# Two one-column buffers fewer, and what lies behind them in a partition moves down by 64 bytes

## The chip, the cores and the metric

The kernel runs on one core of a Trainium2 chip. The metric is the time on the device in microseconds (us) of one execution, for a program that is launched once. Before the change three runs gave 2437.39, 2440.98 and 2445.57 us; the median is 2440.98 us. A profile was taken of one execution, which took 2439.48 us by itself, and its span from the first to the last instruction is 2437.7 us.

## What is computed

The reference is one step of a hybrid encoder with one layer: 2048 prompt tokens and 8 x 16 sample tokens of width 1024, all in float32.

```python
def trunk_layer(x, ...):
    u = rms_norm(x, norm_mix) @ w_in                 # 1024 -> 2564 columns for four mixers
    ya, ... = mixer_ssd(...)                         # chunked state-space scan
    yb      = swa_prompt(...) or swa_sample(...)     # banded attention
    yc, ... = mixer_shortconv(...)
    yd, ... = mixer_conformer(...)                   # 31-tap convolution, layer norm
    x = x + concatenate([ya, yb, yc, yd]) @ w_out
    hf = rms_norm(x, norm_ffn)
    x = x + (silu(hf @ w_gate) * (hf @ w_up)) @ w_down     # 1024 -> 2816 -> 1024
    return x, states
y = rms_norm(x, norm_final)
```

## The kernel before

**Tiles.** The tokens lie along the free axis, the features on the 128 partitions. The 2176 tokens are worked in five chunks of 256, 512, 512, 384 + 128 (the samples) and 384 tokens. Every projection (w_in, w_out, gate, up, down) is a row of matmuls of a 128 x 128 block of weights against an operand of 128 partitions by one chunk.

**Precision.** Weights and operands are split into a high and a low part of a 32-bit type made for matmuls (`split_w` at L202, `split` at L197): ScalarE copies the high part (L204, L199), VectorE subtracts it and leaves the low part (L184). Each product of a block is then three matmuls: high weights times high operand (L239), high weights times low operand (L240), low weights times high operand (L241). TensorE loads its weights anew for each of the three.

**Stages.** Chunks 0 to 2 run through w_in, the mixers, w_out and the feed-forward layer one after the other; the mixers of a chunk are woven between the projections of its neighbours, and the order of instructions on each engine comes from a scheduler that reads the program with its buffers and priorities. The feed-forward layer of chunks 3 and 4 is done together at the end for two halves of 448 tokens (`N` = 448) with seven products in place of eight (`quad`, L1146, and `product`, L1137, whose three matmuls are L1141 to L1143); I call this the quad stage. The products by `w_down` that follow run through `product` too (L1280 and L1292); I call this the down stage.

**Buffers.** Tiles come out of pools with a number of buffers for each tag. The pools on the left of a partition are laid out one behind the other: `cp` (tables, constants and small sums), then `wp` (the raw weights `fr` and the split weights `w`), then the mixer pools `up` and `mp`, in whose place `gp` and `xp` (tiles `g` and part of the operands `hf`) stand at the end of the program. The operands `act`, `h`, `ht`, the rest of `hf` (pool `xq`) and the working tiles `nt`, `ft`, `x2` lie in pools on the right, which are laid out from the other end. A buffer of one column of float32 takes 32 bytes of a partition.

**The place of the change.** `norm1_stats` (L302) makes the sum of squares of a chunk's tokens before its first projection. For chunks 1 to 4 it loads 128 tokens in two halves of 512 features (SyncE, L333), squares them on ScalarE with a sum along the row (L334), and adds the second half's sum `part` to the first's on VectorE (L336; in a profile it stands under the helper's line L184, as `n<-n,n` with one column). `part` is a tile of tag `n1`; `sums` is one of tag `n8`. Each `n1` buffer is free again once its addition has run. This is side work: `weave` puts it among the projections of other chunks.

Of the kernel before, what the change touches and what calls it, by code (L numbers as in the profile page):

```python
# [17 lines left out]
P = 128  # L18
# [100 lines left out]
def stream_step(ctx: ExitStack, tc: tile.TileContext, cfg, x, xr, w_in, w_out, w_gu, w_down, tab, con, dist_p, dist_s,  # L119
# [7 lines left out]
    cp = ctx.enter_context(tc.tile_pool(name="cp", bufs=1))  # L127
# [15 lines left out]
    def mk(pool_, shape, tag, dt=F32, **kw):  # L143
        uid[0] += 1
        return pool_.tile(shape, dt, tag=tag, name=f"{tag}_{uid[0]}", **kw)
# [37 lines left out]
    def tt(out, a, b, op, eng=dve):  # L183
        return eng.tensor_tensor(out=out, in0=a, in1=b, op=op)  # L184
# [59 lines left out]
    def newton(v, r, t, src, n):  # L244
        ts(v, src, 1.0 / n, ALU.mult, EPS, ALU.add)

        ts(r.bitcast(I32), v.bitcast(I32), 1, ALU.logical_shift_right)
        ts(r.bitcast(I32), r.bitcast(I32), -1.0, ALU.mult, float(0x5F1FFFF9), ALU.add)
        stt(t, v, -0.703952253, r, ALU.mult, ALU.mult)
        tt(t, t, r, ALU.mult)  # L250
        stt(r, t, 0.703952253 * 2.38924456, r, ALU.add, ALU.mult)

        stt(t, v, 0.375 ** 0.5, r, ALU.mult, ALU.mult)
        tt(t, t, r, ALU.mult)
        stt(t, t, -1.25 / 0.375 ** 0.5, t, ALU.add, ALU.mult)
        stt(r, t, 1.875, r, ALU.add, ALU.mult)

    def rstd_of(sq, T, n, r=None):

        nb = T // P  # L260
        v, r_, t = (mk(cp, [P, 8], "n8", bufs=9)[:, :nb] for _ in range(3))
        r = r_ if r is None else r
        pc = mk(px, [P, 512], "px")
        for b in range(nb):
            pe.matmul(pc[:, b:b + 1], sq[:, b * P:(b + 1) * P], ones[:, 0:1], start=True, stop=True)
        newton(v, r, t, pc[:, :nb], n)
        return r
# [34 lines left out]
    def norm1_stats(c):  # L302
        T, o = c["T"], c["off"]
        hold = c["i"] == 0 and KT * T <= 4 * TM
        if hold:
            ss = mk(np_, [P, TM], "ns", bufs=1)[:, :T]

            c["x"] = []
            sq = []
            with tc.high_priority(offset=8 * AHEAD):  # L310
                xs = [mk(ap, [P, 2, KT // 4, T], "act") for _ in range(2)]
                for j in range(4):
                    sync.dma_start(xs[j // 2][:, j % 2], x[:, 2 * j:2 * j + 2, o:o + T])
                    c["x"] += [xs[j // 2][:, j % 2, k] for k in range(KT // 4)]
                qs = [mk(ap, [P, 2, KT // 4, T], "act") for _ in range(2)]
                for j in range(4):
                    sq.append(qs[j // 2][:, j % 2])
                    act.activation(sq[j], xs[j // 2][:, j % 2], AF.Square)
                for q in sq[1:]:
                    tt(sq[0], sq[0], q, ALU.add)  # L320
                tt(ss, sq[0][:, 0], sq[0][:, 1], ALU.add)
            yield
            c["r1"] = rstd_of(ss, T, D)
            yield
            return

        nb = T // P
        sums = mk(cp, [P, 8], "n8", bufs=9)[:, :nb]
        for b in range(nb):
            for h in range(2):  # L330
                xt = mk(np_, [P, TM], "nt", bufs=B["nt"])
                part = mk(cp, [P, 1], "n1", bufs=4) if h else sums[:, b:b + 1]
                sync.dma_start(xt, xr[o + b * P:o + (b + 1) * P, h * 512:(h + 1) * 512])  # L333
                act.activation(xt, xt, AF.Square, accum_out=part)  # L334
                if h:
                    tt(sums[:, b:b + 1], sums[:, b:b + 1], part, ALU.add)  # L336
            if b % 2:
                yield
        if nb % 2:
            yield  # L340
        v, r, t = (mk(cp, [P, 8], "n8", bufs=9)[:, :nb] for _ in range(3))
        newton(v, r, t, sums, D)
        c["r1"] = r
        yield
# [620 lines left out]
    def stats1(c):  # L965
        g = norm1_stats(c)
        return twice(g, (c["T"] // P + 1) // 2 + 1)
# [35 lines left out]
    for t in twice(norm1_stats(chunks[0])) + twice(norm1(chunks[0]), 4):  # L1003
        run(t)
# [428 lines left out]
```

## Time and profile before

| what | value |
|---|---|
| median of three runs | 2440.98 us (2437.39 to 2445.57) |
| the profiled execution's own time | 2439.48 us |
| its span, first to last instruction | 2437.7 us |
| mean granted TensorE clock | 0.988 |
| busy: VectorE, ScalarE, GpSimd | 65%, 36%, 6% of the span |
| bytes from and to memory | 324.07 MB read, 91.18 MB written |

A matmul's line in the profile gives the shape of its operand, its count and the mean duration of one. Matmuls overlap: one begins long before the one ahead has ended, so the duration of one (401 ns at 512 columns) is not what it costs. What it costs is the step from one start to the next, which I call the **pace**. It is read from the starts in the timeline, or from a stretch without gaps and the number of matmuls in it.

### The profile page before, as it was taken

The page shows a single profiled execution, that of the slowest core. Times are in us where ns is not written, and L with a number is a line of the kernel's source. Part 1 is how long each engine was busy: PE and PEld are TensorE (multiplying, and loading weights), DVE is VectorE, ACT ScalarE, POOL GpSimd, SP SyncE. Part 2 cuts the span into 40 slices and gives each one's busy share as a digit, 9 for nine tenths or more (in the row PEclk, how much of TensorE's full clock was granted, in tenths as well). Part 3 has the DMA queues.
Part 4 walks back from the last instruction along what each step waited for, and adds up shares of the span by engine and source line. Part 5 has one row for each costly group of instructions (what it writes and reads, how often), then busy time and mean ns, then how long its engine had stood idle before and what let it go on. Part 6 is the DMA issues. An engine that isn't in the chain of part 4 may idle for free.

```text
span 2437.7 us, 32296 instructions
## 1 busy us (share of the span) xinstructions
PE 2373.2 (97%) x12350; PEld 2036.4 (84%) x12350; DVE 1584.0 (65%) x2988; ACT 882.3 (36%) x1494; POOL 146.9 (6%) x266
## 2 busy tenths in 40 slices
PE   6999999999999999997999999999999999999997
PEld 6788999887877778886877788988879999999997
DVE  7897998855784446656573454675687667663324
ACT  5545555533333233323222222233334444442221
POOL 0000000000000000001000000000001000000000
PEclk9999999999999999998999999999999999999998
DMA  6547445567554554555434336653633332338653
GB/s 217 182 163 245 149 156 163 168 234 282 181 185 154 191 173 160 199 208 155 163 135 149 138 121 222 218 172 115 207 108 134 113 130 93 120 121 311 209 186 119
DMA packets 133179, 417.37 MB, mean 171 GB/s; under 512 B 12848, under 2 KB 49616, under 8 KB 115872
## 3 DMA queue, kind: packets, MB, share of 16 engines
q1 hardware_dynamic: 115248, 324.57, 41.1%
q0 software_dynamic: 17776, 90.73, 9.7%
q8 instruction: 97, 1.59, 0.3%
q14 instruction: 58, 0.48, 0.1%
HBM read 324.07 MB, written 91.18 MB: 170 GB/s over the span
## 4 chain that ended last, share of the span: by engine, by line
PE 52%; DMA 2%; DVE 1%; ACT 0%; issue 0%; DVEq 0%; POOL 0%; ACTq 0%; POOLq 0%
PE pm L239 8%; PE pm L240 8%; PE pm L241 8%; PE pm L1141 7%; PE pm L1143 7%; PE pm L1142 7%; PE px L1143 1%; PE px L1141 1%; PE px L1142 1%; DMA o_xc_s<-raw 1%; DVE x L187 0%; DMA act<-kc 0%; DMA raw<-xst 0%; PE px L675 0%; DMA w<-kept 0%; PE px L703 0%
## 5 line engine op out<-in xcount | busy, mean ns | idle before, releaser
L239 PE MATMUL pm<-act,w 128*128 128x512 f32 (+2 forms) x2216 | 808.3, 365 | 6.7 <-ACT act L199 4.1
L240 PE MATMUL pm<-act,w 128*128 128x512 f32 (+2 forms) x2216 | 800.0, 361 | 10.3 <-DVE act L184 10.3
L241 PE MATMUL pm<-act,w 128*128 128x512 f32 (+2 forms) x2216 | 800.0, 361 | 2.3 <-DVE w L184 2.2
L204 ACT ACTIVATE w<-fr 128x1024 fp32r<-128x1024 f32 (+2 forms) x380 | 393.8, 1037 | 909.0 <-PE pm L241 512.4
L184 DVE TENSOR_TENSOR w<-fr,w 128x1024 fp32r<-128x1024 f32 (+2 forms) x380 | 454.2, 1196 | 295.4 <-ACT w L204 294.5
L239 PEld LDWEIGHTS pm<-act,w 128*128 128x128 f32 x2216 | 419.8, 190 | 77.5 <-ACT act L199 5.7
L240 PEld LDWEIGHTS pm<-act,w 128*128 128x128 f32 x2216 | 419.9, 190 | 73.8 <-DVE act L184 11.5
L241 PEld LDWEIGHTS pm<-act,w 128*128 128x128 f32 x2216 | 419.6, 189 | 66.9 <-DVE w L184 3.3
L1141 PE MATMUL pm<-hf,w 128*128 128x448 f32 x616 | 226.2, 367 | 0.0
L1142 PE MATMUL pm<-hf,w 128*128 128x448 f32 x616 | 225.0, 365 | 0.0
L1143 PE MATMUL pm<-hf,w 128*128 128x448 f32 x616 | 224.9, 365 | 0.0
L187 DVE SCALAR_TENSOR_TENSOR mix<-raw,tabh,mix 128x384 f32<-128x384 f32 (+3 forms) x360 | 202.7, 593 | 2.1
L239 PE MATMUL pm<-h,w 128*128 128x512 f32 (+1 forms) x528 | 193.9, 368 | 7.3 <-ACT hf L199 3.3
L240 PE MATMUL pm<-h,w 128*128 128x512 f32 (+1 forms) x528 | 190.7, 362 | 0.1
L241 PE MATMUL pm<-h,w 128*128 128x512 f32 (+1 forms) x528 | 190.6, 362 | 0.0
L184 DVE TENSOR_TENSOR x<-x,pm 128x512 f32<-128x512 f32 (+2 forms) x184 | 107.9, 600 | 76.6 <-PE pm L241 68.8
L187 DVE SCALAR_TENSOR_TENSOR ft<-ft,pm 128x512 f32<-128x512 f32 (+1 forms) x132 | 78.6, 595 | 110.4 <-PE pm L241 91.1
L1143 PEld LDWEIGHTS pm<-hf,w 128*128 128x128 f32 x616 | 115.6, 188 | 10.6
L1141 PEld LDWEIGHTS pm<-hf,w 128*128 128x128 f32 x616 | 115.7, 188 | 9.8 <-ACT g L1155 0.2
L239 PEld LDWEIGHTS pm<-h,w 128*128 128x128 f32 x528 | 101.0, 192 | 27.1 <-ACT hf L199 3.7
L1142 PEld LDWEIGHTS pm<-hf,w 128*128 128x128 f32 x616 | 115.7, 188 | 9.4
L240 PEld LDWEIGHTS pm<-h,w 128*128 128x128 f32 x528 | 101.4, 192 | 16.7 <-issue 0.7
(288 smaller groups left out, 2554.0 us busy)
## 6 DMA issues: line engine op xcount, KB each, us to landing
w<-kept SPq DMA_DIRECT2D x83, 1024.0 KB, 5.2
fr<-w_gu SPq DMA_DIRECT2D x154, 512.0 KB, 3.3
kept<-w POOLq DMA_DIRECT2D x51, 1024.0 KB, 6.4
fr<-w_down SPq DMA_DIRECT2D x84, 512.0 KB, 3.8
fr<-w_in SPq DMA_DIRECT2D x52, 512.0 KB, 4.0
fr<-w_out SPq DMA_DIRECT2D x40, 512.0 KB, 3.4
hm<-h POOLq DMA_DIRECT2D x44, 448.0 KB, 4.4
ht<-hm SPq DMA_DIRECT2D x40, 448.0 KB, 5.3
```

The source lines that it names most:

```text
L184: return eng.tensor_tensor(out=out, in0=a, in1=b, op=op)
L187: return eng.scalar_tensor_tensor(out=out, in0=a, scalar=s, in1=b, op0=op0, op1=op1)
L204: act.activation(d[:, 0, :n], raw, AF.Copy)
L239: pe.matmul(ps[:, :T], wh, o[:, 0, :T], start=(i == 0), stop=False)
L240: pe.matmul(ps[:, :T], wh, o[:, 1, :T], start=False, stop=False)
L241: mm = pe.matmul(ps[:, :T], wl, o[:, 0, :T], start=False, stop=(i == n - 1))
L1141: pe.matmul(ps[:, :N], wh[:, i], a, start=first and i == 0, stop=False, skip_group_check=True)
L1142: pe.matmul(ps[:, :N], wh[:, i], b, start=False, stop=False, skip_group_check=True)
L1143: mm = pe.matmul(ps[:, :N], wl[:, i], a, start=False, stop=(i == n - 1), skip_group_check=True)
```

## The change

```diff
@@ norm1_stats, L332
-                part = mk(cp, [P, 1], "n1", bufs=4) if h else sums[:, b:b + 1]
+                part = mk(cp, [P, 1], "n1", bufs=2) if h else sums[:, b:b + 1]
```

Tag `n1` has two buffers in place of four. That does two things.

**First, every pool behind it on the left begins 64 bytes earlier in each partition**; the right side stays. By the addresses that the build gives the tiles, the beginnings modulo 512 bytes are:

| tile | before | after |
|---|---|---|
| weights `w`, raw weights `fr` | 32 | 480 |
| operands `act`, `h`, `ht`, `hf` of pool `xq` | 480 | 480 |
| operands `hf` of pool `xp` (row blocks 0 and 1 of 4) | 32 | 480 |
| mixer tiles `ut`, `k`, `mix`, `b2` and others | 96 | 32 |

A block of weights is 512 bytes long in a partition, so all blocks of a tile begin at the tile's own place. The low part of an operand lies 2048 bytes behind the high part where a tile holds 512 columns, which is the same place, and 1792 bytes behind it where it holds 448, which is 256 bytes further modulo 512. So before the change the weights and the operands of the first three chunks' projections and of the down stage were 64 bytes apart modulo 512; in the quad stage this held for half of the operands, and the other half began where the weights begin. After it, all of them begin at one place (the low parts at 448 columns 256 bytes off).

**Second, the third partial sum of a chunk must wait for the first addition.** TensorE's, GpSimd's and SyncE's rows are the same as before. On ScalarE one row moves, in the statistics of chunk 4, which run beside the w_in projections of chunk 3 and the feed-forward layer of chunk 2. The two pieces show ScalarE there; `nt_1689` is the working tile of the third block, `n1_1690` its partial sum, `pk` and `ut_1584` belong to the time steps of the scan, `w` are weights, `h` and `ft` belong to the feed-forward layer, and `ut_1603` is the projection v on its way to a transpose.

```order
 L199 ACTIVATE h_1581_10260<-ft_1577_10226 128x512 [waits DVE_49]
 L475 ACTIVATE ut_1584_10306<-pm_1583_10281,tab_1_84 128x512 [waits PE_49]
-L334 ACTIVATE nt_1689_11083,n1_1690_11084<-nt_1689_11083 128x512 [waits DMAHW5_49,Activation_49]
 L476 ACTIVATE ut_1585_10307<-ut_1584_10306 128x512 [waits Activation_49]
 L477 ACTIVATE ut_1585_10307<-ut_1585_10307 128x512 [waits Activation_49]
```

The square of the third block stood ahead of the chain of the time steps; here it is gone, and a few rows further down on the same engine it comes again:

```order
 L199 ACTIVATE h_1597_10430<-ft_1591_10367 128x512 [waits DVE_49]
 L911 ACTIVATE ft_1600_10460<-pm_1599_10435 128x512 [waits DVE_49,PE_49]
+L334 ACTIVATE nt_1689_11083,n1_1690_11084<-nt_1689_11083 128x512 [waits DMAHW5_49,DVE_49]
 L204 ACTIVATE w_1615_10585<-fr_1614_10583 128x1024 [waits DMAHW3_49,DMAHW4_49,DMAHW2_49,PE_49]
 L534 ACTIVATE ut_1603_10506<-pm_1602_10481 128x512
```

It now stands ahead of the split of the weights `w_1615` and of the copy of v, and waits for VectorE, which must have run the addition of the first partial sum. On VectorE, in the same place of the program, the additions of the first two partial sums stand just above the next piece, in both kernels at the same rows; that of the third moves down:

```order
 L368 COPY raw_1670_10953<-hg1_14_104 128x30
 L191 TENSOR_SCALAR raw_1670_10953<-raw_1670_10953 128x8x30
-L184 TENSOR_TENSOR n8_1647_10813<-n8_1647_10813,n1_1690_11084 128x1
 L368 COPY raw_1710_11210<-hs0_11_101 128x2
 L192 TENSOR_SCALAR mix_1672_10963<-raw_1670_10953,tabh_5_92,tab_1_84 128x128
+L187 SCALAR_TENSOR_TENSOR mix_1672_10963<-raw_1670_10953,tabh_5_92,mix_1672_10963 128x128
+L184 TENSOR_TENSOR n8_1647_10813<-n8_1647_10813,n1_1690_11084 128x1
+L187 SCALAR_TENSOR_TENSOR mix_1672_10963<-raw_1670_10953,tabh_5_92,mix_1672_10963 128x128
 L192 TENSOR_SCALAR n8_1726_11340<-n8_1647_10813 128x3
```

The third addition comes three rows later. Elsewhere on VectorE some taps of a convolution and steps of the scan change places among themselves. In the statistics of the other chunks the square of a later block now waits for an addition as well, at an unchanged place in the order.

## The prediction

> **What bounds the kernel now.** I read the page first, for which engine is full:
>
> ```profile
> span 2437.7 us, 32296 instructions
> PE 2373.2 (97%) x12350; PEld 2036.4 (84%) x12350; DVE 1584.0 (65%) x2988; ACT 882.3 (36%) x1494; POOL 146.9 (6%) x266
> PE   6999999999999999997999999999999999999997
> PEclk9999999999999999998999999999999999999998
> ```
>
> TensorE (PE) is busy in nearly every slice at nearly its full granted clock; nothing else comes near. The table of waits says the same from the other side:
>
> ```profile
> ACT w L204 <- PE pm L241: 512.4, 162, 11.4
> ```
>
> The split of the weights waits 512 us in all for TensorE to give a buffer back, so weights come early. Next, the groups by line with shapes kept apart, for how many matmuls of each width there are:
>
> ```profile
> L239 PE MATMUL pm<-act,w 128*128 128x512 f32 x1400 | 561.8, 401 | 4.6 <-ACT act L199 2.9 <-DMA w<-kept 1.7
> L239 PE MATMUL pm<-h,w 128*128 128x512 f32 x352 | 143.3, 407 | 3.3 <-ACT hf L199 3.3
> L239 PE MATMUL pm<-act,w 128*128 128x384 f32 x232 | 79.4, 342 | 0.0
> L239 PE MATMUL pm<-act,w 128*128 128x256 f32 x584 | 167.0, 287 | 2.1 <-ACT act L199 1.2 <-ACT w L204 0.5 <-ACT pk L498 0.4
> L239 PE MATMUL pm<-h,w 128*128 128x256 f32 x176 | 50.6, 290 | 4.0 <-DVE ft L187 1.8 <-DVE x L184 1.7 <-ACT h L199 0.5
> L1143 PE MATMUL pm<-hf,w 128*128 128x448 f32 x616 | 224.9, 365 | 0.0
> L1143 PE MATMUL px<-ht,w 128*128 128x448 f32 x160 | 58.8, 368 | 0.0
> L1143 PE MATMUL pm<-ht,w 128*128 128x448 f32 x160 | 58.8, 367 | 0.0
> L1143 PE MATMUL pm<-h,w 128*128 128x448 f32 x16 | 5.9, 366 | 0.0
> L1143 PE MATMUL px<-h,w 128*128 128x448 f32 x16 | 5.8, 365 | 0.0
> ```
>
> Each line has two sisters with the same count (L240 and L241, L1141 and L1142). So there are 3 x (1400 + 352) = 5256 matmuls of 512 columns, 696 of 384, 2280 of 256, 1848 of 448 in the quad stage and 3 x 352 = 1056 of 448 in the down stage. Idle time ahead of them is a few us in all.
>
> Last, seven gapless stretches, by the view of windows: start and end, the length, TensorE busy, the number of matmuls that it touches, clock, DMA share and GB/s. A window also counts a matmul that still runs at its left edge; the steps from its first to its last start are 354, 95, 22, 133, 60, 479 and 1653.
>
> ```profile
> 562.14:644.74 82.60, 82.60 (x356) 1.00 0.62 221
> 1528.36:1545.14 16.78, 16.78 (x97) 1.00 0.70 201
> 1601.22:1605.03 3.81, 3.81 (x23) 1.00 0.61 252
> 169.38:184.48 15.10, 15.10 (x136) 1.00 0.43 140
> 336.34:343.40 7.06, 7.06 (x62) 1.00 0.47 155
> 2214.03:2310.89 96.86, 96.86 (x480) 1.00 0.79 262
> 1866.83:2203.85 337.02, 337.02 (x1654) 1.00 0.36 120
> ```
>
> Length by steps gives the paces: 512 columns 233.3 ns; 384 columns 176.6 in one stretch and 173.2 in another; 256 columns 113.5 and 117.7; 448 columns 202.2 in the down stage and 203.9 in the quad stage. So one width has **two paces** at the same clock. Counts by paces (with the mean of the two at 384 and 256) give 1226 + 122 + 264 + 377 + 214 = 2203 us, 90% of the span. A change of pace goes to the end of the kernel whole.
>
> **The change part by part.** The sum is made against the profiled execution's own 2439.5 us, which lies 1.5 us under the median of the runs.
>
> *The wait on ScalarE* (chunk 4's statistics). These rows of the timeline are of ScalarE, VectorE and TensorE in turn:
>
> ```profile
> 1149.37 0.63 ACT L334 ACTIVATE nt<-nt 128x512 f32<-128x512 f32 x1 [3.57 <-DMA nt<-xr]
> ...
> 1172.67 1.06 ACT L204 ACTIVATE w<-fr 128x1024 fp32r<-128x1024 f32 x1 [2.49 <-PE pm L241]
> 1173.63 0.58 ACT L534 ACTIVATE ut<-pm 128x512 f32<-128x512 f32 x1
> ```
>
> ```profile
> 1173.95 0.23 DVE L184 TENSOR_TENSOR n<-n,n 128x1 f32<-128x1 f32 x2
> ```
>
> ```profile
> 1174.34 0.38 PE L543 MATMUL px<-con,ut 128*128 128x128 f32 x2
> ```
>
> The square that moves (first row) will stand just ahead of the split at 1172.67 and wait for the first of the two additions, which begins at 1173.95 and is done by about 1174.1. VectorE's rows up to there are as many as before, so that time stays. The square holds ScalarE 0.63 us; the split begins at about 1174.75, **2.1 us late**, and the copy of v behind it as late. TensorE takes v's transposes at 1174.34, 0.13 us after the copy ends (1173.63 + 0.58), so it will stand for 2.1 us, and all behind it in its queue moves. The split itself is of weights two units on, which hides it. ScalarE gains 3.57 + 0.63 us at 1149 in exchange, but TensorE had no gap there to give back:
>
> ```profile
> 1134.91:1174.10 39.19, 39.19 (x169) 1.00 0.63 209
> ```
>
> 168 steps at 233.3. Ends of the term: 0 (VectorE comes earlier by the 2.1) and 2.1; I take +2.1. The other added waits cost nothing: there the addition two sums back is done before the square begins, by the places of both in the order.
>
> *The place of weights and operands at 448 columns.* The quad stage has both cases side by side: in each product the first six matmuls take operands that begin where the weights begin (pool `xp`), the last six take operands 64 bytes apart (`xq`). The starts of the 1st, 7th and of the next product's 1st matmul:
>
> ```profile
> 1900.66 0.37 PE L1141 MATMUL pm<-hf,w 128*128 128x448 f32 x1
> ...
> 1901.90 0.37 PE L1141 MATMUL pm<-hf,w 128*128 128x448 f32 x1
> ...
> 1903.11 0.37 PE L1141 MATMUL pm<-hf,w 128*128 128x448 f32 x1
> ```
>
> 1.24 us for six at one place, 206.7 ns each; 1.21 us for six 64 apart, 201.7. Over the whole stretch: the mean is 203.9, and if the half that is 64 apart goes at the down stage's 202.2 (all 64 apart there), the other half goes at 205.6. Against it stands the very first quad, 1826.00 to 1842.78:
>
> ```profile
> 1826.00 0.36 PE L1141 MATMUL pm<-hf,w 128*128 128x448 f32 x1
> ...
> 1827.21 0.36 PE L1141 MATMUL pm<-hf,w 128*128 128x448 f32 x1
> ...
> 1828.42 0.36 PE L1141 MATMUL pm<-hf,w 128*128 128x448 f32 x1
> ```
>
> Here both halves take 1.21 us: one place can also go at the fast pace. So the place doesn't force the slow pace; it allows it, and which it is was set by what stood before the stretch. After the change all 448-wide matmuls are at one place. I take 205.6, since 1653 steps show it and the fast stretch has some 80: 1848 x (205.6 - 203.9) + 1056 x (205.6 - 202.2) = 3.1 + 3.6 = **+6.7 us**. Ends: all at 202.2, -3.1 us; all at 206.7, 5.2 + 4.8 = +10 us.
>
> *The place at 512, 384 and 256 columns.* All of these are 64 apart before, at one place after; no row shows that. The fast paces lie on a line: 113.5, 173.2, 233.3, some 60 ns for each 128 columns. The slow ones lie on another: 117.7, 176.6, and at 448 it gives 206.1, which is what one place showed there. So 512 columns go on the fast line now, and the slow line would be 235.5 there, +2.2 ns. Below, I bound by the step between the two paces at 256, -4.2; above by +4.2. That is from -22 to +22 us for 5256 matmuls, and at 256 from -9.6 to +9.6 for 2280; 384 has under 700 and is within 2 us. I take **0**: the row nearest to a 512-wide matmul is its own width's, and both long stretches of it quoted here, 570 us apart, have this one pace.
>
> A rule to weigh here: the Trainium skill, "SBUF — State Buffer", section "Who interferes with whom", gives TensorE two independent read ports, one for the operand and one for the weights; I read it as saying that it doesn't matter where the two lie. By it the term of place would be 0 and the sum 2441.6; the 206.7 against 201.7 above speaks against it, the 1.21 against 1.21 for it.
>
> Sum: 2439.5 + 2.1 + 6.7 + 0 = **2448.3 us**.
>
> **The rivals.**
>
> *All widths take the slow line.* If one place lets the slow pace in at every width as at 448, 512 columns pay 2.2 x 5256 = 11.6 us and 256 columns half of their 9.6, 4.8 us: 2448.3 + 16.4 = 2464.7. For it: the line fits three widths to 0.5 ns. Against it: the slow pace also occurs at 256 and 384 columns, 64 apart, so it isn't the place alone that makes it.
>
> *Place plays no part.* Then the two paces come from what stood ahead of a stretch alone, as the first quad suggests, and only the wait is left: 2439.5 + 2.1 = 2441.6. Against it: 1653 steps in a row with the two halves of each product apart.
>
> *One place is faster* (the other side). The weights of the next matmul are read while the operand of this one streams; if at one place the two run past each other with one delay less in each matmul, 512 columns gain what lies between the two paces at 256, 4.2 x 5256 = 22.1 us, 256 columns half of their 9.6, and 448 columns go at 202.2 (-3.1): 2441.6 - 22.1 - 4.8 - 3.1 = 2411.6. For it: 202.2 at 448 is already 1 ns under the fast line (203.3), so a place can do better than the line. Against it: no stretch at one place does better than 202. It decides from a gain of 0.9 ns on each 512-wide matmul (4.8 us), with the other terms at 2.1 - 3.1.
>
> **How the numbers follow.** Forecast 0.30, slow line at all widths 0.25, no part 0.20, one place faster 0.25. Against the median 2441.0, 0.3% is 7.3 us, which is about what a measurement of this kernel can tell from no change: under 2433.7 is faster, over 2448.3 slower. The forecast lies on that line, so I halve it: faster 0.25, same 0.20 + 0.15 = 0.35, slower 0.25 + 0.15 = 0.40. All terms at their low ends give 2405, all at their high ends 2483; with a tenth left out at each side the range is 2411 to 2474.
>
> **What would show it.** In the profile after: the pace at 448 columns in the quad stage and the down stage, about 205.6 in both if I am right, 202 if the place plays no part; the pace of the long 512-wide stretch near 562 us, 233.3 by the forecast, 235.5 by the slow line, 229 by the fast rival; a stand of about 2 us ahead of the transposes L543 near 1174 us. What would make me wrong most is the 512-wide pace: each 1 ns of it is 5.3 us, and no row of before shows it at one place.

## The result, and the profile after

| | before | after |
|---|---|---|
| median of four runs each | 2439.18 us (2436.48 to 2445.57) | 2417.66 us (2412.88 to 2418.89) |
| the profiled execution's own time | 2439.48 us | 2412.88 us |
| its span | 2437.7 us | 2411.1 us |

The ratio of after to before is 0.9904, 95% interval 0.9880 to 0.9929. The change makes the kernel faster by about 1%; I had forecast 2448.3 us, 0.3% slower. The time lies inside the range that I gave, near its lower end, on the side of the third rival. The profiled execution after the change is the fastest of its four: the two profiled executions lie 26.6 us apart, the medians 21.5, and what follows accounts for the profiled two. One execution of k3_both_lower below, at a granted clock of 0.654, took 3327.78 us and is in no ratio.

The page of the kernel after, the same four lines as before:

```profile
span 2411.1 us, 32296 instructions
PE 2343.1 (97%) x12350; PEld 2038.6 (85%) x12350; DVE 1582.2 (66%) x2988; ACT 882.4 (37%) x1494; POOL 147.3 (6%) x266
PE   6999999999999999998999999999999999999997
PEclk9999999999999999998999999999999999999998
```

TensorE (PE) still bounds the kernel in nearly every slice at the same clock, and the counts are the same. Of the busy times only its own has shrunk by more than 2 us, by 30.1. So the time went out of the matmuls themselves. The groups by line with shapes kept apart say which:

```profile
L239 PE MATMUL pm<-act,w 128*128 128x512 f32 x1400 | 553.1, 395 | 5.0 <-ACT act L199 3.2 <-DMA w<-kept 1.7
L239 PE MATMUL pm<-act,w 128*128 128x256 f32 x584 | 169.0, 291 | 1.8 <-ACT act L199 1.1 <-ACT w L204 0.4 <-ACT pk L498 0.3
```

At 512 columns the mean fell from 401 to 395 ns, at 256 it rose from 287 to 291. The paces are read from gapless stretches by the view of windows (start and end, length, TensorE busy, matmuls touched, clock, DMA share, GB/s), at least one of each width. The first and the sixth are those of 82.60 and 337.02 us before. From the first start to the last there are 354, 155, 94, 187, 83, 1653 and 479 steps:

```profile
564.26:644.55 80.29, 80.29 (x356) 1.00 0.63 226
166.11:184.71 18.60, 18.60 (x157) 1.00 0.44 142
405.08:416.36 11.28, 11.28 (x96) 1.00 0.55 184
1682.97:1715.40 32.43, 32.43 (x189) 1.00 0.64 208
1824.07:1841.21 17.14, 17.14 (x85) 1.00 0.47 169
1841.47:2176.71 335.24, 335.24 (x1654) 1.00 0.36 120
2186.92:2284.00 97.08, 97.08 (x481) 1.00 0.79 260
```

Length by steps: 512 columns 226.8 ns (233.3 before); 256 columns 120.0 in both stretches (113.5 and 117.7 in the two of before); 384 columns 173.4 (176.6 and 173.2 before); 448 columns 206.5 in a short stretch, then 202.8 in the long one of the quad stage and 202.7 in the down stage.

To see what each width is worth over the whole kernel, I summed over the trace the step from each matmul's start to the next one's start, by the width of the first, in us. A step counts the stand (TensorE's idle time) that may lie in it; some 20 us ahead of the first start and behind the last one are in no row. The last four columns belong to the experiments below. Each column is one execution: before and k1_wait_only, which go at the same pace at 512 columns, differ by 3.3 us there and by 5.5 us in their spans, so a few us between two columns say little.

| width | before | after | k1_wait_only | k2_place_only | k4_256_apart | k5_448_64 |
|---|---|---|---|---|---|---|
| 512 (5256) | 1270.9 | 1240.1 | 1267.6 | 1239.1 | 1237.6 | 1238.0 |
| 448 (2904) | 594.5 | 593.5 | 594.5 | 593.3 | 597.3 | 586.5 |
| 256 (2280) | 293.8 | 301.1 | 290.9 | 299.3 | 294.9 | 292.7 |
| 384 (696) | 124.8 | 123.0 | 124.8 | 125.4 | 123.1 | 123.4 |
| others | 134.1 | 133.7 | 134.8 | 133.1 | 131.7 | 134.8 |
| span | 2437.7 | 2411.1 | 2432.2 | 2409.9 | 2404.3 | 2395.1 |

From before to after: -30.8, -1.0, +7.3, -1.8 and -0.4, together -26.7 us; that this is the span's -26.6 must be so, since the steps make up the span.

The added wait is there too. The timeline after, ScalarE, VectorE and TensorE in turn (start, duration, instruction, in brackets the idle time ahead and what ended it):

```profile
1162.08 0.63 ACT L334 ACTIVATE nt<-nt 128x512 f32<-128x512 f32 x1 [4.23 <-DVE n L184]
...
1162.71 1.04 ACT L204 ACTIVATE w<-fr 128x1024 fp32r<-128x1024 f32 x1
1163.65 0.58 ACT L534 ACTIVATE ut<-pm 128x512 f32<-128x512 f32 x1
```

```profile
1161.89 0.22 DVE L184 TENSOR_TENSOR n<-n,n 128x1 f32<-128x1 f32 x2
```

```profile
1160.85 0.39 PE L240 MATMUL pm<-act,w 128*128 128x512 f32 x1
1164.28 0.66 PE L543 MATMUL px<-con,ut 128*128 128x128 f32 x4 [3.05 <-ACT ut L534]
```

ScalarE stands 4.23 us ahead of the moved square, until VectorE's addition; the split and the copy of v follow late, and TensorE stands 3.05 us ahead of the transposes L543.

### The profile page after: what moved, and what is told of

It is laid out like the page before. It is cut to its first block, busy times and chain, and to the rows that moved or that the text cites. A ratio compares the mean times of both kernels' runs of the same rounds, so it can differ in the third digit from the quotient of the medians.

```text
span 2411.1 us, 32296 instructions
## 1 busy us (share of the span) xinstructions
PE 2343.1 (97%) x12350; PEld 2038.6 (85%) x12350; DVE 1582.2 (66%) x2988; ACT 882.4 (37%) x1494; POOL 147.3 (6%) x266
## 4 chain that ended last, share of the span: by engine, by line
PE 49%; DVE 3%; DMA 2%; ACT 0%; issue 0%; DVEq 0%; POOL 0%; ACTq 0%; POOLq 0%
PE pm L239 7%; PE pm L240 7%; PE pm L241 7%; PE pm L1141 7%; PE pm L1142 7%; PE pm L1143 7%; PE px L1141 1%; PE px L1143 1%; PE px L1142 1%; DMA nt<-xr 1%; DVE mix L187 1%; DMA o_xc_s<-raw 1%; DVE x L187 0%; DMA act<-kc 0%; DMA raw<-xst 0%
## 5 line engine op out<-in xcount | busy, mean ns | idle before, releaser
L240 PEld LDWEIGHTS pm<-act,w 128*128 128x128 f32 x2216 | 420.7, 190 | 65.2 <-DVE act L184 10.8
L239 PE MATMUL pm<-h,w 128*128 128x512 f32 (+1 forms) x528 | 191.4, 363 | 7.3 <-ACT hf L199 3.3
L241 PE MATMUL pm<-h,w 128*128 128x512 f32 (+1 forms) x528 | 188.6, 358 | 0.0
L240 PE MATMUL pm<-h,w 128*128 128x512 f32 (+1 forms) x528 | 188.4, 357 | 0.0
```

The costliest lines, as they stand in the source:

```text
L239: pe.matmul(ps[:, :T], wh, o[:, 0, :T], start=(i == 0), stop=False)
L240: pe.matmul(ps[:, :T], wh, o[:, 1, :T], start=False, stop=False)
L241: mm = pe.matmul(ps[:, :T], wl, o[:, 0, :T], start=False, stop=(i == n - 1))
```

## The experiments

The question: is it the place of weights against operands, an absolute place, or the moved order that gives the 6.5 ns at 512 columns? The first three kernels take the two effects of the change apart. All ratios are to the kernel before.

**k1_wait_only: the order of the change, the places of before.** In the kernel after, a wider tile behind the two buffers takes up the 64 bytes:

```diff
-    A = mk(cp, [P, 1], "A")
+    A = mk(cp, [P, 17], "A")[:, 0:1]
```

> The order and the added waits of the change, with the places of before: the tile A takes 96 bytes in place of 32, so weights begin at 32 and operands at 480 modulo 512 again. Theory of place (what the 512-wide matmuls gain comes from weights and operands that begin at one place): the long 512-wide stretch near 562 us goes at 233.3 ns as before, 256-wide ones at 113 to 118, the stand ahead of the transposes L543 near 1174 us stays at about 3 us, and the time is before plus 3, about 2442 us, ratio 1.001. Theory of order (the gain comes from the moved rows and waits): 226.8 ns, 2418 us, ratio 0.990.

Measured: 2440.08 us, ratio 1.0013 (1.0001 to 1.0024). In its timeline ScalarE waits as in the kernel after, and the window of the long 512-wide stretch (354 steps) shows the old pace:

```profile
1169.46 0.63 ACT L334 ACTIVATE nt<-nt 128x512 f32<-128x512 f32 x1 [4.23 <-DVE n L184]
```

```profile
559.30:641.91 82.61, 82.61 (x356) 1.00 0.62 221
```

233.4 ns. So neither the moved rows nor the wait bring any of the gain; alone they cost 0.2 to 5.8 us. The stand of TensorE ahead of the transposes was expected at about 3 us and came to 1.5, by the view of L543 from 1150 to 1185 us:

```profile
L543 PE MATMUL px<-con,ut x4: 273/273/328, 1171.7 to 1172.1; 128*128 128x128 f32 x4
its engine sat idle before it (us, times) until:
  ACT ut L534: 1.5, 1
```

**k2_place_only: the places of the change, without the wait at chunk 4.** Three buffers for `n1`, and `A` becomes a column of `tabh` (lines against the kernel before):

```diff
-    th = mk(cp, [P, n_half], "tabh")
+    th = mk(cp, [P, n_half + 1], "tabh")
...
-    A = mk(cp, [P, 1], "A")
+    A = th[:, n_half:n_half + 1]
...
-                part = mk(cp, [P, 1], "n1", bufs=4) if h else sums[:, b:b + 1]
+                part = mk(cp, [P, 1], "n1", bufs=3) if h else sums[:, b:b + 1]
```

> The places of the change without its wait at the statistics of chunk 4: n1 has three buffers and A is a column of the tile tabh, so that weights begin at 480 modulo 512 as after. Theory of place: 226.8 ns at 512 columns, about 120 at 256, no stand ahead of L543 near 1174 us beyond that of before, and the time is after less about 3, some 2414.5 us, ratio 0.989. Theory of order: 233.3 ns and the time of before, ratio 1.000.

Measured: 2411.85 us, ratio 0.9904 (0.9888 to 0.9920). Windows of the 512-wide stretch (354 steps) and of a 256-wide one (155):

```profile
561.26:641.55 80.29, 80.29 (x355) 1.00 0.62 226
164.81:183.40 18.59, 18.59 (x156) 1.00 0.42 143
```

226.8 and 119.9 ns, as after. The place alone gives the whole gain, and the rise at 256 columns too. That the wait's 3 us are saved against the kernel after can't be told by the ratios, whose intervals overlap; by the timeline TensorE has no idle time ahead of L543 there.

**k3_both_lower and k3_again: weights where the change put them, operands 64 bytes lower.** In the kernel after, a pad on the right moves the operands to 416, so the two are 64 apart again:

```diff
+    pad = ctx.enter_context(tc.tile_pool(name="pad", bufs=1, side="right")).tile([P, 16], F32, tag="pad", name="pad")
...
+    nc.gpsimd.memset(pad, 0.0)
```

> The change, and a pad of 64 bytes on the right, so that act, h, ht and the hf of pool xq begin at 416 modulo 512; weights stay at 480, where the change put them. Weights and operands are 64 apart again, by the same sign as before. Theory of the relative place: paces of before (233.3 ns at 512 columns near 562 us, 113 to 118 at 256), about 2442 us, ratio 1.001. Theory of the absolute place of the weights: paces of after (226.8, 120), about 2418 us, ratio 0.990. Theory of the absolute place of the operands: a pace that neither kernel shows.

> The kernel of k3_both_lower once more, for a profile at full clock (the clock granted in the first one's profile was 0.65, so its paces can't be set beside the others). By its time, 1.0013 of before, and the theory of the relative place: 233.3 ns in the long 512-wide stretch near 562 us, 113 to 118 at 256 columns, though the weights stand at 480 as after the change. By the theory of the absolute place of the weights 226.8 and 120.

Measured: 2440.20 us, ratio 1.0013 (1.0003 to 1.0023), the time of k1_wait_only; k3_again took 2434.78 us in one run, beside 2435.02 for the kernel before. The paces are from the profile of k3_again, windows of the 512-wide stretch (354 steps) and of two 256-wide ones (132 and 94):

```profile
559.99:642.59 82.60, 82.60 (x356) 1.00 0.62 221
165.43:180.41 14.98, 14.98 (x134) 1.00 0.40 141
387.53:398.60 11.07, 11.07 (x96) 1.00 0.55 179
```

233.3, 113.5 and 117.8 ns: all paces of before, with the weights at their new place. It is the distance between the two that sets these paces, not where the weights lie.

**m1_places: matmuls alone.** The layer is left out. Each stretch repeats, for blocks `k` of weights and an operand `oo` columns into its buffer:

```python
for i in range(0, steps, 3):
    wh, wl = (wt[:, s, wo + k * P:wo + k * P + m] for s in range(2))
    a, b = buf[:, k, oo:oo + n], buf[:, k, oo + low:oo + low + n]
    pe.matmul(ps, wh, a, ...); pe.matmul(ps, wh, b, ...); pe.matmul(ps, wl, a, ...)
```

> Only matmuls, in stretches of 48 of one width, three for each block as in the projections; all of the layer is left out and zeros are written. Weights begin at 128 modulo 512; the operand begins 4 x d bytes further, for d = 112 (64 bytes less, as before the change), 0 (one place, as after), 64, 16, 96, 32, 120, 80, 8, 48, 104, 24, 72, 56, 40, 88 columns, then 112 and 0 again, at 512, 256, 384 and 448 columns; then d = 112 and 0 with the weights moved by 16, 112 and 8 columns. Theory of the relative place: at 512 columns 233.3 ns at d = 112 and 226.8 at d = 0, wherever the weights are; at 256 columns 113.5 or 117.7 at d = 112 and about 120 at d = 0; between these d a curve that no run shows yet. Theory of absolute places: the pace moves with the weights. Theory of order: one pace for each width.

Windows over the last 30 steps of a stretch. First 512 columns, the weights at 128: 64 bytes apart, at one place; then the weights at 192: 64 apart, at one place. Then 256 columns: 64 apart twice, at one place. Last 448 columns: at one place, and the operand 64 bytes behind the weights:

```profile
230.09:237.09 7.00, 7.00 (x31) 1.00 0.00 0
242.22:249.02 6.80, 6.80 (x31) 1.00 0.01 2
729.95:736.95 7.00, 7.00 (x31) 1.00 0.00 0
766.46:773.26 6.80, 6.80 (x31) 1.00 0.00 0
252.26:255.80 3.54, 3.54 (x32) 1.00 0.00 0
355.69:359.09 3.40, 3.40 (x32) 1.00 0.00 0
362.04:365.64 3.60, 3.60 (x32) 1.00 0.00 0
547.72:553.80 6.08, 6.08 (x31) 1.00 0.00 0
569.06:575.06 6.00, 6.00 (x32) 1.00 0.01 3
```

7.00 us for 30 steps are 233.3 ns, 6.80 are 226.7, wherever the weights stand; 3.54, 3.40 and 3.60 are 118, 113.3 and 120.0; 6.08 and 6.00 are 202.7 and 200.0. These are the kernels' paces to a fraction of a ns, with little else running and DMA idle. The first expectation, the relative place, holds at all points but the first stretch of the run, where TensorE still waited for its operands and which gives no pace; the other two fall. More of the curve, in ns, by how far the operand begins behind the weights (two distances 256 bytes apart in each cell, each read over the last 30 steps):

| columns | 0 / 256 B | 32 / 288 B | 64 / 320 B | 128 / 384 B | 192 / 448 B |
|---|---|---|---|---|---|
| 512 | 226.7 / 226.7 | 233.3 / 233.3 | 228.9 / 228.9 | 232.3 / 232.3 | 233.3 / 233.3 |
| 448 | 202.7 / 202.7 | 206.7 / 200.0 | 200.0 / 200.0 | 204.0 / 204.0 | 202.2 / 202.2 |
| 384 | 173.3 / 173.3 | 173.3 / 173.3 | 173.3 / 173.3 | 176.0 / 176.0 | 176.7 / 174.7 |
| 256 | 120.0 / 120.0 | 116.8 / 116.7 | 117.8 / 117.8 | 118.7 / 118.7 | 113.3 / 117.8, then 113.3 |

Two things can be read from it. The period is 256 bytes, not 512, but for a few points with two paces. And each width has a best distance of its own: 0 at 512 columns, 64 bytes (and some others) at 448, 192 or 448 bytes at 256. Before the change the distance was 448 for nearly all: the best for the fewer 256-wide matmuls where they fall into the faster of its two paces, and among the worst for the many 512-wide ones.

**m2_high_low: high and low part apart from each other.** The same kernel, with the low part's place set by itself; again only matmuls. A pair gives how many columns of 4 bytes the high and the low part begin behind the weights.

> Only matmuls again; all of the layer is left out and zeros are written. Weights begin at 128 modulo 512; the high part of the operand begins 0, 8, ..., 56 columns further and the low part, by itself, 0, 8, ..., 56 columns further (modulo 256 bytes, since places 256 bytes apart gave the same pace at 512 columns in the run before: 226.67 at 0 and 64 columns, 233.33 at 48 and 112). 64 pairs at each of 512, 448, 256 and 384 columns, 48 matmuls each. Theory of the relative place: the pair (0, 0) gives 226.7, 202.7, 120.0 and 173.3 ns, and (48, 48) gives 233.3, 202.2, 113.3 or 117.8 and 174.7 to 176.7. If each matmul pays by its own operand's place alone, a pair costs two thirds of the high part's own pace and a third of the low part's, so no pair is under the best equal pair. If a matmul's step hangs on the place of the one ahead of it too, some mixed pair is better or worse than both. Theory of order: one pace for each width.

Windows over the last 30 steps: 512 columns at (0, 48) and (48, 0), 448 columns at (16, 16), 256 columns at (48, 48) and (48, 56):

```profile
109.20:116.06 6.86, 6.86 (x31) 1.00 0.00 0
619.29:626.32 7.03, 7.03 (x32) 1.00 0.00 0
1006.25:1012.25 6.00, 6.00 (x32) 1.00 0.00 0
1847.55:1850.95 3.40, 3.40 (x33) 1.00 0.00 0
1853.88:1857.45 3.57, 3.57 (x33) 1.00 0.00 0
```

By the starts, (0, 48) goes at 228.9 ns, the two thirds and one third of 226.7 and 233.3, but (48, 0) at 234.4, above both, where that theory gives 231.1; and (0, 16) goes at 232.0, above the 226.7 and 228.9 of its two places. So a matmul's step doesn't hang on its own operand's place alone; that of a neighbour counts as well. Each pair was read once. None of the 64 pairs goes under the best equal pair: 228.9 is the least of the mixed ones at 512 columns, 200.0 at 448, 116.7 at 256 (equal: 226.7 in m1_places, 200.0, 113.3). The pair (0, 0) at 512 columns stood first in the run, where TensorE still waited for its operands, and gives no pace. Two equal pairs missed what was expected of them: 206.7 at (0, 0) with 448 columns (202.7 in m1_places), and 173.3 at (48, 48) with 384 (174.7 to 176.7).

**k4_256_apart: a distance for each width, first step.** k2_place_only, and chunk 0 keeps its operands 192 bytes into each half of its tiles (the other two tiles of tag `act` likewise):

```diff
+    at = lambda d, c: d[:, :, 48:] if c["T"] == 2 * P else d
...
-            d = mk(ap, [P, 2, TM], "act", F32R)
+            d = at(mk(ap, [P, 2, TM], "act", F32R), c)
...
-            d = mk(hp, [P, 2, TM], "h", F32R)
+            d = at(mk(hp, [P, 2, TM], "h", F32R), c)
```

> The kernel of k2_place_only (places of the change, no added wait at the statistics of chunk 4), and chunk 0, whose tiles use 256 of 512 columns, keeps its operands 48 columns (192 bytes) into each half of the tile. Rows of all engines stand as in k2_place_only. Theory of the relative place: 512-wide matmuls stay at 226.8 ns, 256-wide ones leave about 119.8 and go at 113.3 (the pace of the pair (48, 48)) or 117.8 where they fall into the slower one; 2280 x 2.0 to 6.5 = 4.6 to 14.8 us, so 2397 to 2407 us against the 2411.85 of k2_place_only, ratio 0.984 to 0.988. Theory of order or of absolute places: no difference to k2_place_only.

Measured: 2407.21 us, ratio 0.9887 (0.9865 to 0.9908). Windows of two 256-wide stretches (94 and 133 steps) and of the down stage (479):

```profile
386.89:397.56 10.67, 10.67 (x95) 1.00 0.56 182
163.86:179.52 15.66, 15.66 (x134) 1.00 0.39 135
2176.38:2275.38 99.00, 99.00 (x481) 1.00 0.76 257
```

113.5 and 117.7 ns at 256 columns, as expected; the time just misses the 2397 to 2407 us. The 2280 matmuls gave back only 4.4 us in the table of steps, not the 10 us of their mean gapless steps (119.8 to 115.5 ns, steps of up to 130 ns): what lies above those steps, stands and short stretches, rose from 26 to 32 us. And the down stage, whose places this edit doesn't touch, went at 206.7 ns in place of 202.7, and took back 4.0: at 448 columns one place has **two paces** too. By its ratio alone this kernel can't be told from k2_place_only.

**k5_448_64: second step.** k4_256_apart, with the operands at 448 columns 64 bytes behind the weights:

```diff
-    late = {}
+    late, pads = {}, [mk(xp, [P, 16], "pad", bufs=1)]
...
-                d = mk(hp, [P, 2, TM], "h", F32R)[:, :, :N]
+                d = mk(hp, [P, 2, TM], "h", F32R)[:, :, 16:16 + N]
...
+    pads.append(mk(pq, [P, 112], "pad"))
```

(the last line stands ahead of the pools `xq` and `ht` on the right, each in a pool of its own).

> k4_256_apart, and the operands at 448 columns (hf, ht, and h at the end) begin 64 bytes behind the weights' place modulo 512 (pads of 64 and 448 bytes, and h 16 columns into its tile), where the stretches of matmuls alone went at 200.0 ns in place of 202.7. By it 2904 x 2.7 = 7.8 us less than k4_256_apart, about 2388 to 2399 us; a pace of 200.0 in the long stretch of the quad stage and in the down stage. If the quad stage, where something else reads and writes beside it, does not keep that pace, no difference to k4_256_apart.

Measured: 2398.64 us, ratio 0.9839 (0.9823 to 0.9854). Windows of 1066 steps of the quad stage and of the down stage (479):

```profile
1948.70:2161.90 213.20, 213.20 (x1067) 1.00 0.35 121
2172.04:2267.84 95.80, 95.80 (x480) 1.00 0.79 268
```

200.0 ns in both. The 448-wide steps took 10.8 us less than in k4_256_apart, more than the 7.8 expected, since the down stage had gone at 206.7 there. The interval of the ratio lies under that of the change itself: this version beats both kernels, by about 1.6% against before.

**m3_which_pair: which weights does the operand meet?** Matmuls alone; here the weights move on from one matmul to the next, and the operand with them.

```python
for j in range(steps):
    k, s = j % 8, step * j % 64
    w = wt[:, j // 8 % 2, k * P + s:(k + 1) * P + s]
    o = (s + r) % 64
    pe.matmul(ps, w, buf[:, k, o:o + n], ...)
```

> Only matmuls; all of the layer is left out and zeros are written. One after the other, each with its own weights and operand. Weights move on by step columns (0, 0, 16 or 48, modulo 64) from one matmul to the next, and each operand begins r = 0, 16, 32 or 48 columns behind its own weights' place (modulo 64 columns). So the distance to its own weights is r, to the next matmul's weights r - step, to the last one's r + step, each the same in all of a stretch. With step 0 at 512 columns: 226.7, 228.9, 232.3, 233.3 ns for r = 0, 16, 32, 48, as in the first run of matmuls alone. Theory A (the operand that streams meets the weights of the next matmul, which are loaded meanwhile): with step 16 the 226.7 stands at r = 16, with step 48 at r = 48. Theory B (its own weights): 226.7 at r = 0 with each step. Theory C (the last one's): at r = 48 with step 16, at r = 16 with step 48. At 256 columns the 120.0 of r = 0 moves in the same way.

Windows over the last 30 steps at 512 columns: step 0 with r = 0 and 48; step 16 with r = 0, 16, 32, 48; step 48 with r = 48:

```profile
87.86:94.66 6.80, 6.80 (x31) 1.00 0.00 0
124.05:131.05 7.00, 7.00 (x31) 1.00 0.00 0
136.23:143.15 6.92, 6.92 (x31) 1.00 0.00 0
148.33:155.27 6.94, 6.94 (x31) 1.00 0.01 2
160.48:167.45 6.97, 6.97 (x32) 1.00 0.00 0
172.61:179.53 6.92, 6.92 (x31) 1.00 0.00 0
221.15:228.14 6.99, 6.99 (x32) 1.00 0.00 0
```

With step 0 the two ends are 226.7 and 233.3 again (the very first stretch, which began with waits, ran at 232.5 over its last 30 steps and at 226.7 over its last 18). With step 16 all four lie between 230.6 and 232.3, with step 48 between 231.7 and 233.0: 226.7 stands nowhere. At 256 columns the 120.0 of r = 0 stands at r = 48 with step 16 and nowhere with step 48 (117.3 to 119.3). All three theories miss. At 512 columns the fast pace needed both, the same place from matmul to matmul and the right distance; against which weights the distance counts stays open.

## Why the prediction was wrong

**What bounds the kernel** held: TensorE's busy time fell by 30.1 us and the span by 26.6, and most of what lies between is its stand of 3.05 us. So the change of pace went to the end of the kernel whole.

**The step that failed is the place at 512 columns,** which I took as 0 with a bound of 4.2 ns. It is -6.5 ns in the long stretch and -30.8 us over the kernel with the added wait in it, outside the -22 that I had set as the low end. Two things in my step were wrong. I took the row nearest by width, though every 512-wide row of before was 64 apart, so it said nothing of one place. And I drew the line of the paces 64 apart (113.5, 173.2, 233.3, 60 ns for each 128 columns) through to one place. The runs show another line there: 120.0, 173.3, 226.7 ns, so 53.3 ns for each 128 columns and a larger fixed part (only 448 columns, at 202.7, lie off it). One place gains with width and loses at 256 columns; the bound, borrowed from the two paces at 256, could not hold. That the range held the time is luck: this term fell 8.7 us below its low end, while those at 256 and 448 columns came out above theirs. (A tenth of the way in from 2405 and 2483 is 2413 and 2475, not the 2411 and 2474 that I gave; the time lies in both.)

**256 columns**: the pace rose by 2.3 to 6.5 ns in the stretches, the total by 7.3 us. The total lay within the bound of 9.6, the taken 0 did not. **384 columns**: -1.8 us, within the 2 allowed.

**448 columns**: I took 205.6 ns at one place, +6.7 us; it came to -1.0. That the place doesn't force the slow pace but allows it was right, and the kernel after has both, 206.5 for 83 steps and 202.8 for the next 1653. What I read as the mark of one place was one of its two paces. k4_256_apart shows the other case, a whole down stage at 206.7.

**The wait on ScalarE**: right in place and mechanism, too small in size, 2.1 us predicted and 3.05 found. I let VectorE keep its time against TensorE; but its addition came only 12.06 us earlier (1173.95 to 1161.89), while TensorE's last matmul ahead of the transposes ended at about 1161.2, 13.1 us ahead of the old start of L543. At the old pace, in k1_wait_only, the stand was 1.5 us, less than I had summed: here the faster TensorE made its wait on the other engines longer.

**The rivals.** That the place plays no part falls with k1_wait_only and k2_place_only, the slow line at all widths with the 226.8. The fast rival was right in its sign and near in its sum, 2411.6, but by terms that err both ways: it had -22.1 at 512 columns (-30.8 found, with a stand of 3.05 in it) and -4.8 at 256 (+7.3 found). Its story, that the weights of the next matmul run past the operand, is not shown: m3_which_pair speaks against each single pairing. That the weights' place is one side of it is shown by m1_places, where operand and weights moved together keep the pace.

The rule that I weighed, from the Trainium skill, "SBUF — State Buffer", section "Who interferes with whom", of two independent read ports for TensorE, can't be read as I read it: m1_places moves only the operand by 64 bytes, with no DMA and little else at work, and the pace goes from 233.3 to 226.7 ns. The page speaks of ports and not of places; that it makes the place indifferent was my reading. The Trainium skill, "TensorE: Matmul & The Clock Gate", section "Back-to-back issue gap", lets the gap of a matmul by itself on a warm TensorE grow with the columns divided by 2.4, in ns: 53.3 for each 128. The slope agrees with these streams at one place (53.3 from 256 to 512 columns) and not 64 apart (60).

## What to carry to other kernels

Where matmuls with a weight load each fill TensorE, the distance between weights and operand within a partition, modulo 256 bytes, was worth up to 3% at 512 columns and 6% at 256 in these runs, and any edit of a small tile in front can change it for the whole kernel; so compare the addresses before explaining such an edit by its waits. A stretch of 48 matmuls alone measures the pace of a distance to a fraction of a ns, if it is repeated, since there can be two; and each width wants its own distance. In a forecast, a term that no row of the kernel before can show, on the most frequent instruction, should carry most of the width and no preferred sign; a row of the same width under the other condition is not evidence for it.

## What the runs showed of the hardware

- The paces of 512, 384 and 256 columns at one place, and of 448 columns 64 bytes behind, lie on one line: 226.7, 173.3, 120.0 and 200.0 ns are 13.3 ns and 53.3 for each 128 columns. At 512 columns other distances pay up to 6.7 ns on top, by the table of m1_places; at 256 columns one place is the slowest of that table, and the others go under the line, down to 113.3.
- The same places can have two steady paces: 113.3 and 117.8 at 256 columns, 64 apart; 202.7 and 206.5 to 206.7 at 448 columns, at one place. At 448 columns a stretch kept the one it had fallen into for hundreds of matmuls. What picks it was not found.
- With weights of 32 columns in place of 128, m1_places showed 231.7 ns for 512 columns at distances of 448, 0 and 256 bytes alike: with a quarter of the weights to load, these places made no difference, and the pace was not the best one either.
